# A depthwise convolution of width 31: taps on four engines, or Fourier transforms of spans of tokens on TensorE

## The chip, the cores and the metric

The kernel runs on one core of one Trainium2 chip. Times are device microseconds of one execution of the whole program. TensorE is called PE below (PEld is its weight load), VectorE is DVE, ScalarE is ACT, GpSimd is POOL, and SP is the queue that issues most transfers.

## What is computed

A two-layer encoder block over 1,024 tokens of 1,024 channels, in float32. Layer 0 mixes tokens by a convolution module, layer 1 by a gated linear recurrence, and each is followed by a squared-ReLU MLP. The change is in layer 0's convolution module:

```python
def conformer_conv(h, w_in, dw_w, dw_b, ln_g, ln_b, w_out):
    a, gate = jnp.split(h @ w_in, 2, axis=-1)
    u = a * jax.nn.sigmoid(gate)
    pad = CONV_WIDTH // 2                 # CONV_WIDTH = 31
    y = lax.conv_general_dilated(
        u, dw_w[:, None, :], window_strides=(1,), padding=[(pad, pad)],
        dimension_numbers=("NWC", "WIO", "NWC"), feature_group_count=D_MODEL)
    y = y + dw_b
    y = jax.nn.silu(layer_norm(y, ln_g, ln_b))
    return y @ w_out
# in the layer: h = rms_norm(x) * (1 + sc1) + sh1;  x = x + g1 * conformer_conv(h, ...)
#               sh1, sc1, g1, sh2, sc2, g2 = split(silu(c) @ ada_w + ada_b, 6)
```

## The kernel before

Activations lie with channels on the 128 partitions and tokens along the free axis, so x is 8 tiles of 128x1024. Every large product splits both operands into a float32r high part and the rest (`hi`/`lo`, `wh`/`wl`), and does three matmuls for one: `wh*hi`, `wh*lo`, `wl*hi`. Weights come by the SP queue into a ring of four 128x1024 tiles (`raw`), ACT rounds `wh` (line 190), and DVE, or POOL for the keys in `PW`, subtracts to get `wl` (line 194). Both go to a ring of six tiles, that is three pairs.

`start` loads x, makes the first norm and the modulation, and leaves h as 16 tiles of 128x2x512 (8 blocks of channels, two halves of 512 tokens). `conv_layer` then goes over 8 blocks of 128 channels. `conv_in(b)` makes both halves of a and gate, with weights stationary and h moving (512 columns), and writes u as three sequences: even tokens, odd tokens, and their sum (line 729, POOL), which is a two-phase split of the filter into three filters of half the length. While `conv_in(b + 1)` runs on PE, `conv_pe` and `conv_taps` apply block b's taps: some by a diagonal stationary matrix on PE (line 756, its diagonal made by ACT at line 755), the even ones by ACT's scale (line 770) and POOL's add (line 772), the odd ones and the sum's as a chain of multiply-adds on DVE (line 782, into the SBUF tile `g` and into the PSUM tile `aux`). y is put together at lines 796 and 798, and its mean over channels is summed on PE into two banks (line 800).

When all 8 blocks are done the layer norm follows: `conv_center`, `conv_rms` (squares, sums, Newton steps, spread over partitions by line 480), `conv_swish` with the split into z; then `out_proj` of the first half of the tokens, the second half's swish, and `out_proj` of the second half in `rest`, with layer 0's MLP behind it. The modulation's parts are products with ada_w: most are done as POOL products (line 382) that ACT sums (line 387), one 128x1024 tile for 128 outputs; g1, part (0, 2), is done on PE by `ada_pe` (line 409). Part (0, 4) is spread over the first `out_proj`, (0, 3) follows it.

Instructions are put in order by a planner from the program's order, priorities and estimated costs, engine by engine; `keep_in_program_order` pins one to its place. PSUM has 3 banks for `acc`, 3 for `aux` and 2 for `mu` in this layer.

Of the kernel before, what the change touches and what calls it, by code (L numbers as in the profile page):

```python
# [13 lines left out]
P = 128  # L14
D = 1024
# [7 lines left out]
NE = KW // 2 + 1  # L23
UW = T // 2 + PAD
# [16 lines left out]
TAPS = [(2, 16, 0)] * 6 + [(3, 16, 5), (16, 13, 0)]  # L41
# [30 lines left out]
PW = [("ci", 0, 0), ("ci", 0, 1), ("co", 3), ("co", 4)]  # L72
ADA_PE = [(0, 2)]
# [12 lines left out]
class K:  # L86
    def __init__(self, tc, ins, out):
        self.tc, self.nc, self.ins, self.out = tc, tc.nc, ins, out
        self.uid = self.ndg = 0
        self.pin = self.pins = self.stay = False  # L90
        self.turn = {"acc": 0, "aux": 0}
        self.pq = self.kept = None
# [22 lines left out]
    def plan(self):  # L115
# [12 lines left out]
        for b in range(NB):  # L128
            L.append((("ci", b, 0), [col(w_in, b)], "std"))
            L.append((("ci", b, 1), [col(w_in, NB + b)], "std"))  # L130
# [30 lines left out]
    def fetch(self, upto):  # L161
        while self.fnext <= min(upto, len(self.wlist) - 1):
            key, aps, _ = self.wlist[self.fnext]
            self.raws[key] = []
            for ap in aps:
                raw = self.raw()
                self.nc.sync.dma_start(out=raw.rearrange("p (k n) -> p k n", n=ap.shape[-1]), in_=ap)
                self.raws[key].append(raw)
            self.fnext += 1

    def prep(self, upto):
        while self.wnext <= min(upto, len(self.wlist) - 1):
# [3 lines left out]
            self.wready[key] = {"std": self.prep_std, "spill": self.prep_std, "again": self.prep_again,  # L176
                                "pair": self.prep_pair}[kind](key, aps, raws, kind)
# [7 lines left out]
    def prep_std(self, key, aps, raws, kind):  # L185
# [4 lines left out]
        i = nc.scalar.copy(out=wh, in_=raw)  # L190
        if self.stay:
            self.tc.keep_in_program_order(i)
        eng = nc.gpsimd if key in PW else nc.vector
        i = eng.tensor_tensor(out=wl, in0=raw, in1=wh.bitcast(F32), op=ALU.subtract)
        if self.stay and eng is nc.gpsimd:
            self.tc.keep_in_program_order(i)
# [108 lines left out]
    def setup_late(self):  # L305

        nc, cp = self.nc, self.cp
        self.dw = cp.tile([P, NB, KW], F32, name="dw")
        nc.sync.dma_start(out=self.dw, in_=self.ins["dw"].rearrange("p (b k) -> p b k", k=KW))
        self.dws = cp.tile([P, NB, NE], F32, name="dws")  # L310
        nc.vector.tensor_tensor(out=self.dws[:, :, 0:NE - 1], in0=self.dw[:, :, 0:KW - 1:2], in1=self.dw[:, :, 1::2],
                                op=ALU.add)
        nc.vector.tensor_copy(out=self.dws[:, :, NE - 1:], in_=self.dw[:, :, KW - 1:])

# [53 lines left out]
    def ada(self, layer, part, cond, tile, eng="vector", late=False):  # L368

        nc = self.nc  # L370
        for b in range(NB):
# [9 lines left out]
            else:  # L381
                i = nc.gpsimd.tensor_tensor(out=raw, in0=raw, in1=cond, op=ALU.mult)  # L382
                if self.stay:
                    self.tc.keep_in_program_order(i)
# [13 lines left out]

    def ada_pe(self, layer, part, steps):


        nc = self.nc
        w = self.ins["ada_w"].rearrange("(k p) n -> p k n", p=P)
        ps = [self.acc() for _ in range(2)]
        for k in range(NB):
            raw = self.hp.tile([P, D], F32, tag="h", name=self.nm("raw"))
            nc.sync.dma_start(out=raw, in_=w[:, k, ADA_PE.index((layer, part)) * D:][:, 0:D])
            for j in range(2):
                m = nc.tensor.matmul(ps[j][0:1], self.cond[:, k:k + 1], raw[:, self.hs(j)],
                                     start=(k == 0), stop=(k == NB - 1))  # L410
                self.tc.keep_in_program_order(m)
            if k + 1 in steps:
                yield
        yield
        rows = []
        for j in range(2):
            row = self.t512("row")[0:1]
            nc.scalar.copy(out=row, in_=ps[j][0:1])
            rows += [row[:, i * P:(i + 1) * P] for i in range(4)]
        ps = self.aux()  # L420
        for b in range(NB):
            nc.tensor.matmul(ps[:, b:b + 1], rows[b], self.ones_c[0:1], start=True, stop=True)
        self.ada_done(layer, part, ps[:, 0:NB], 0, NB)
        yield
# [132 lines left out]
    def mod_split(self, layer, n, b, t):  # L557
        shift = self.gcol(layer, 3 * n, b)
        h = self.hp.tile([P, 2, H], F32R, tag="h", name=self.nm("h"))
# [5 lines left out]
    def mod_split_pool(self, layer, n, s, b, r):  # L565

        nc = self.nc
        h = self.hp.tile([P, 2, H], F32R, tag="h", name=self.nm("h"))
# [101 lines left out]
    def start(self):  # L670
# [13 lines left out]
        h = [[], []]  # L684

        def block(b):
            for s in range(2):
                if s:
                    h[s].append(self.mod_split_pool(0, 0, s, b, rs[s]))
                else:  # L690
                    t, _ = self.mod_scale(0, 0, s, b, rs[s])
                    h[s].append(self.mod_split(0, 0, b, t)[0])
# [17 lines left out]
    def conv_in(self, b, h):  # L710


        nc, sp = self.nc, self.sp
        u = sp.tile([P, 3, UW], F32, tag="u", name=self.nm("u"))
        for i, n in ((0, PAD // 2), (1, PAD // 2 + 1)):
            nc.gpsimd.memset(u[:, i, 0:n], 0.0)
            nc.gpsimd.memset(u[:, i, n + H:], 0.0)
        ws = [self.weights(("ci", b, i), 2 if b else 0) for i in range(2)]
        for s in range(2):
            pa, pg = self.acc(), self.mu.tile([P, H], F32, tag="mu", name=self.nm("mu")) if b == 0 and s else self.acc()  # L720
            self.mm3(pa, ws[0], slice(0, P), h[s])
            self.mm3(pg, ws[1], slice(0, P), h[s])
            sg = self.t512("sg")
            nc.scalar.activation(out=sg, in_=pg, func=AF.Sigmoid)
            uv = self.view(u, PAD // 2 + s * H // 2, [[1, H // 2], [UW + 1, 2]])
            nc.vector.tensor_tensor(out=uv, in0=pa.rearrange("p (m i) -> p m i", i=2),
                                    in1=sg.rearrange("p (m i) -> p m i", i=2), op=ALU.mult)
            if s:
                nc.gpsimd.tensor_tensor(out=u[:, 2], in0=u[:, 0], in1=u[:, 1], op=ALU.add)
            yield u  # L730

    def spare(self, i):

        return self.x[i][:, self.hs(1)]

    def conv_pe(self, b, u):  # L740

        nc, sp = self.nc, self.sp
        n0, n1, late = TAPS[b]
        banks = []
        for x, w, lo, hi, more in ((u[:, 2], self.dws[:, b], 0, n0, late), (u[:, 0], self.dw[:, b, 0::2], n1, NE, 0)):
            ps = self.aux() if hi > lo else None
            self.diag(ps, x, w, lo, hi, True, not more)
            banks.append(ps)
        return banks

    def diag(self, ps, x, w, lo, hi, start, stop):
        for j in range(lo, hi):
            self.ndg += 1
            d = self.spare(2 + self.ndg % 8 // 4)[:, self.ndg % 4 * P:(self.ndg % 4 + 1) * P]
            self.nc.scalar.activation(out=d, in_=self.ident, func=AF.Copy, scale=w[:, j:j + 1])
# [826 lines left out]
```

## Time and profile before

| | us |
|---|---|
| median of 3 runs | 2584.30 (2583.52 to 2584.58) |
| the profiled execution | 2588.68 |
| its span, first to last instruction | 2586.9 |
| PE busy in the span | 2411.8 (93%) |
| DVE busy | 1955.2 (76%) |
| POOL busy | 1130.6 (44%) |
| ACT busy | 1044.7 (40%) |
| mean granted PE clock | 0.973 |

The span is read by stages, since the shares of the whole hide that different engines set the pace in different stages. A matmul's duration in the trace overlaps with the next one's; what a matmul costs a full PE is the distance from its start to the next one's start. A float32 (not float32r) matmul stands in the trace as two instructions.

### The profile page before, as it was taken

What the parts mean: (1) busy time and instruction counts of PE and PEld (TensorE: products, weight loads), DVE (VectorE), ACT (ScalarE), POOL (GpSimd) and SP (SyncE); (2) the same over time, 40 slices, a digit from 0 to 9 for tenths busy, and PEclk for the clock granted to TensorE, in tenths of its full rate; (3) what the DMA queues carried; (4) which work ended last, traced back from release to release, by engine and by line L of the source; (5) the groups of instructions that cost most, each with busy time, mean ns of one, the idle gap of its engine ahead of it and who ended that gap; (6) DMA issues with size and microseconds to landing.
All of it is one profiled execution on the core that took longest, in us unless ns stands there. A gap on an engine that the chain in (4) does not pass through costs nothing.

```text
span 2586.9 us, 31297 instructions
## 1 busy us (share of the span) xinstructions
PE 2411.8 (93%) x11538; PEld 1974.0 (76%) x11538; DVE 1955.2 (76%) x2547; ACT 1044.7 (40%) x1738; POOL 1130.6 (44%) x647
## 2 busy tenths in 40 slices
PE   3888778889899999999999999999998999999998
PEld 2666536667688878888889898988877888888887
DVE  8999989896576789765776767768669766686565
ACT  5544435343333444444433434442424333333443
POOL 4678755466576588211111101111016666564421
PEclk9998889989999999999999999999998999999999
DMA  7111422424444946552211112122522444574554
GB/s 248 41 33 33 155 104 82 164 94 159 159 159 168 339 174 227 197 179 90 74 58 50 58 58 66 58 66 65 204 98 93 157 153 139 207 271 169 188 179 154
DMA packets 214974, 347.25 MB, mean 134 GB/s; under 512 B 13091, under 2 KB 117795, under 8 KB 214822
## 3 DMA queue, kind: packets, MB, share of 16 engines
q1 hardware_dynamic: 213094, 343.17, 38.9%
q8 instruction: 90, 1.47, 0.2%
q10 hardware_dynamic: 1728, 2.10, 0.2%
q14 instruction: 62, 0.51, 0.1%
HBM read 267.62 MB, written 77.60 MB: 133 GB/s over the span
## 4 chain that ended last, share of the span: by engine, by line
PE 71%; DVE 19%; issue 4%; POOL 3%; DMA 2%; ACT 0%; SPq 0%; POOLq 0%; DVEq 0%; ACTq 0%
PE acc L267 16%; DVE g L782 5%; PE acc L956 5%; PE acc L957 5%; PE acc L952 5%; PE acc L1058 4%; PE acc L1053 4%; PE aux L1224 4%; PE acc L1057 4%; PE aux L1053 3%; PE aux L1058 3%; PE aux L1057 3%; DVE aux L782 2%; PE acc L257 2%; PE acc L258 2%
## 5 line engine op out<-in xcount | busy, mean ns | idle before, releaser
L382 POOL TENSOR_TENSOR raw<-raw,cond 128x1024 f32<-128x1024 f32 x56 | 160.2, 2863 | 549.4 <-DMA raw<-in_ada_t 466.9
L267 PE MATMUL acc<-h,wh 128*128 128x512 f32 x1024 | 328.7, 397 | 0.0
L222 DVE TENSOR_TENSOR wp<-raw,wp 128x512 fp32r<-128x512 f32 x192 | 198.7, 1043 | 115.0 <-ACT wp L221 114.5
L952 PE MATMUL acc<-h,wp 128*128 128x512 f32 x640 | 254.4, 403 | 11.4 <-ACT wp L221 8.3
L956 PE MATMUL acc<-h,wp 128*128 128x512 f32 x640 | 256.8, 402 | 7.6 <-DVE h L629 7.6
L957 PE MATMUL acc<-h,wp 128*128 128x512 f32 x640 | 255.3, 404 | 5.4 <-DVE wp L222 5.4
L221 ACT CAST wp<-raw 128x512 fp32r<-128x512 f32 x192 | 117.2, 620 | 353.9 <-PE acc L957 183.9
L1041 DVE TENSOR_TENSOR o<-hold,o 128x1024 fp32r<-128x1024 f32 x80 | 156.2, 1953 | 83.8 <-ACT o L1040 76.8
L267 PEld LDWEIGHTS acc<-h,wh 128*128 128x128 f32 x1024 | 190.5, 189 | 37.0
L267 PE MATMUL acc<-h,wl 128*128 128x512 f32 x512 | 202.9, 397 | 0.0
L1058 PE MATMUL acc<-o,o 128*128 128x512 f32 (+1 forms) x512 | 195.2, 383 | 2.9 <-DVE o L1041 2.9
L1057 PE MATMUL acc<-o,o 128*128 128x512 f32 (+1 forms) x512 | 194.2, 379 | 0.0
L1053 PE MATMUL acc<-o,o 128*128 128x512 f32 (+1 forms) x512 | 194.0, 382 | 0.0
L772 POOL TENSOR_TENSOR x<-x,x 128x512 f32<-128x512 f32 x117 | 183.3, 1566 | 8.2
L1041 DVE TENSOR_TENSOR o<-c,o 128x1024 fp32r<-128x1024 f32 x96 | 174.6, 1819 | 12.6 <-ACT o L1040 12.5
L1053 PE MATMUL aux<-o,o 128*128 128x512 f32 (+1 forms) x448 | 171.0, 382 | 0.4 <-ACT o L1040 0.4
L1057 PE MATMUL aux<-o,o 128*128 128x512 f32 (+1 forms) x448 | 169.1, 377 | 0.0
L1058 PE MATMUL aux<-o,o 128*128 128x512 f32 (+1 forms) x448 | 167.1, 380 | 0.6 <-DVE o L1041 0.6
L952 PEld LDWEIGHTS acc<-h,wp 128*128 128x128 f32 x640 | 123.9, 194 | 43.3 <-ACT wp L221 10.9
L1040 ACT CAST o<-hold 128x1024 fp32r<-128x1024 f32 x80 | 83.9, 1049 | 172.1 <-issue 86.5
L957 PEld LDWEIGHTS acc<-h,wp 128*128 128x128 f32 x640 | 123.5, 193 | 37.0 <-DVE wp L222 8.9
L956 PEld LDWEIGHTS acc<-h,wp 128*128 128x128 f32 x640 | 123.3, 193 | 36.6 <-DVE h L629 8.4
(257 smaller groups left out, 6232.5 us busy)
## 6 DMA issues: line engine op xcount, KB each, us to landing
raw<-in_mlp_w SPq DMA_DIRECT2D x144, 512.0 KB, 4.4
c<-hid SPq DMA_DIRECT2D x112, 512.0 KB, 3.5
hid<-c SPq DMA_DIRECT2D x128, 256.0 KB, 3.1
raw<-in_ada_t SPq DMA_DIRECT2D x56, 512.0 KB, 3.7
hid<-t SPq DMA_DIRECT2D x96, 256.0 KB, 2.9
raw<-in_hgrn_w_in SPq DMA_DIRECT2D x40, 512.0 KB, 3.8
aw<-in_ada_t SPq DMA_DIRECT2D x32, 512.0 KB, 7.9
hold<-in_mlp_w SPq DMA_DIRECT2D x32, 512.0 KB, 7.8
```

Source lines behind the costliest of these rows:

```text
L222: nc.vector.tensor_tensor(out=lo, in0=a, in1=hi.bitcast(F32), op=ALU.subtract)
L267: m = self.nc.tensor.matmul(ps, a, b, start=(k == 0 and i == 0), stop=(k == n - 1 and i == 2))
L382: i = nc.gpsimd.tensor_tensor(out=raw, in0=raw, in1=cond, op=ALU.mult)
L772: nc.gpsimd.tensor_tensor(out=e, in0=e, in1=p, op=ALU.add)
L782: nc.vector.scalar_tensor_tensor(out=out, in0=x[:, j:j + n], scalar=w[:, j:j + 1], in1=out, op0=ALU.mult, op1=ALU.add)
L952: m = nc.tensor.matmul(ps, wh, hi, start=(k == 0 and i not in (3, 6, 7)), stop=False, skip_group_check=True)
L956: nc.tensor.matmul(ps, wh, lo, start=False, stop=False, skip_group_check=True)
L957: nc.tensor.matmul(ps, wl, hi, start=False, stop=(k == KH - 1), skip_group_check=True)
L1041: nc.vector.tensor_tensor(out=lo, in0=src, in1=hi.bitcast(F32), op=ALU.subtract)
L1053: m = nc.tensor.matmul(ps[j], wh[:, c], hi, start=first, stop=False, skip_group_check=True)
L1057: nc.tensor.matmul(ps[j], wh[:, c], lo, start=False, stop=False, skip_group_check=True)
L1058: nc.tensor.matmul(ps[j], wl[:, c], hi, start=False, stop=stop, skip_group_check=True)
```

## The change

The tap loops and their three sequences go. Tokens of u are now on partitions, in 8 tiles of 128 tokens, and channels go in 4 groups of 256 (`G`). For a half of 512 tokens, three spans (`NWIN`) of 171 output tokens (`DV`) are each computed from 201 input tokens by a transform of length 202 (`DN`), whose 102 frequencies lie on partitions: cosine and sine sums by matmuls with fixed matrices (`F`), a complex product with the filter's transform (`W`), and an inverse by matmuls with fixed matrices (`Gm`), after which y is again channels by tokens.

`conv_in(ps, g)` has h stationary and the weights moving (256 columns of a and 256 of gate), and holds one bank for each 128 tokens. It runs in two passes over all 1,024 x 2,048 weights: pass 0 for tokens 0 to 639 (5 tiles), pass 1 for 640 to 1023 (3 tiles). The weights are therefore loaded, rounded and subtracted twice. u of tiles 3 and 4 is kept for pass 1. `forward` and `backward` of a group are put between the four quarters (`kp`) of the next group's `conv_in`. The first half's layer norm and swish (`conv_norm`) go one step per quarter into pass 1; the second half's go into the first `out_proj`. The matrices F and the kept u take the place of x in SBUF, so all of x is loaded again behind the last `forward`. `ada_pe` goes; parts (0, 2), (0, 4) and (0, 3) all become POOL products through the ring `raw`, in pass 1 and the first `out_proj`.

The diff, cut:

```diff
-TAPS = [(2, 16, 0)] * 6 + [(3, 16, 5), (16, 13, 0)]
+DN = 202
+DV = 171
+NWIN = 3
+G = 256
+NG = D // G
+PASS = [range(0, 5), range(5, 8)]
+KEPT = [3, 4]
+SHIFTS = [(j, t) for j in range(NWIN) for t in range(-1, 5)
+          if any(0 <= P * t + p - DV * j + PAD < DV + KW - 1 for p in range(P))]
...
-PW = [("ci", 0, 0), ("ci", 0, 1), ("co", 3), ("co", 4)]
-ADA_PE = [(0, 2)]
+PW = [("ci", 0, 0, 0), ("ci", 0, 0, 1), ("co", 3), ("co", 4)]
...
+        for ps in range(len(PASS)):
+            for g in range(NG):
+                for k in range(0, NB, 2):
+                    L.append((("ci", ps, g, k // 2), [w_in[:, k + i, :, g * G:(g + 1) * G] for i in range(2)], "whole"))
...
     def setup_late(self):
+        xr = [self.xp.tile([P, T], F32R, tag="x", name=self.nm("xr")) for _ in range(NB)]
+        self.F = [xr[i][:, 0:H].rearrange("p (e c f) -> p e c f", e=2, c=2) for i in range(n)]
+        self.ukept = [t[:, H:].rearrange("p (e n) -> p e n", e=2) for t in xr]
+        for i in range(n + 2):
+            if i % 4 == 0:
+                raw = self.raw()
...
+            nc.scalar.copy(out=hi, in_=src)
+            nc.vector.tensor_tensor(out=lo, in0=src, in1=hi.bitcast(F32), op=ALU.subtract)
...
+    def conv_in(self, ps, g, h, U):
+        banks = {t: self.acc() if i < 3 else self.mbank() for i, t in enumerate(PASS[ps])}
+        for kp in range(NB // 2):
+            wh, wl = self.weights(("ci", ps, g, kp))
+            for k in range(2 * kp, 2 * kp + 2):
+                a, b = (w[:, self.hs(k % 2)] for w in (wh, wl))
+                for t, bank in banks.items():
+                    c = slice(t % 4 * P, (t % 4 + 1) * P)
+                    hi, lo = (h[t // 4][k][:, e, c] for e in range(2))
+                    nc.tensor.matmul(bank, hi, a, start=(k == 0), stop=False)
+                    nc.tensor.matmul(bank, hi, b, start=False, stop=False)
+                    nc.tensor.matmul(bank, lo, a, start=False, stop=(k == NB - 1))
+            if kp < NB // 2 - 1:
+                yield
+        for t, bank in banks.items():
+            w = self.t512("u")
+            nc.scalar.activation(out=w[:, 0:G], in_=bank[:, G:], func=AF.Sigmoid)
+            nc.vector.tensor_tensor(out=w[:, G:], in0=bank[:, 0:G], in1=w[:, 0:G], op=ALU.mult)
...
+            nc.scalar.copy(out=u[:, 0], in_=w[:, G:])
+            nc.vector.tensor_tensor(out=u[:, 1], in0=w[:, G:], in1=u[:, 0].bitcast(F32), op=ALU.subtract)
...
+    def forward(self, s, g, U):
+        for j in range(NWIN):
+            ps = self.aux()
+            ts = [(i, 4 * s + t) for i, (w, t) in enumerate(SHIFTS) if w == j and 0 <= 4 * s + t < NB]
+            for c in range(2):
...
+                    nc.tensor.matmul(out, fh, hi, start=(n == 0), stop=False)
+                    nc.tensor.matmul(out, fh, lo, start=False, stop=False)
+                    nc.tensor.matmul(out, fl, hi, start=False, stop=(n == len(ts) - 1))
...
+            for out, c in ((p, 0), (q, 1)):
+                w = self.W[:, c:c + 1, g * G:(g + 1) * G].broadcast_to([P, 2, G])
+                nc.vector.tensor_tensor(out=out, in0=sp, in1=w, op=ALU.mult)
+            for c, op in ((0, ALU.add), (1, ALU.subtract)):
+                nc.gpsimd.tensor_tensor(out=p[:, c], in0=p[:, c], in1=q[:, 1 - c], op=op)
...
+            self.split(y, p)
...
+    def backward(self, s, g, Y, ys, sums):
+        banks = [self.aux() for _ in range(3)]
+        for j in range(NWIN):
+            for b in range(G // P):
+                mm = [(Y[j][:, e, c, b * P:(b + 1) * P], self.Gm[:, f, c]) for c in range(2)
+                      for e, f in ((0, 0), (0, 1), (1, 0))]
...
+            if 0 < n < NB - 2:
+                nc.gpsimd.tensor_tensor(out=sums[0], in0=sums[0] if n > 1 else ys[0], in1=y, op=ALU.add)
...
+    def conv_norm(self, ys, sums, s, z):
+        for i, t in enumerate((sums[0], ys[NB - 2], ys[NB - 1])):
+            nc.tensor.matmul(mu, self.ones_d, t, start=(i == 0), stop=(i == 2))
...
     def conv_layer(self, h):
+                for ps in range(2):
+                    for g in range(NG):
+                        ci = self.conv_in(ps, g, h, U)
...
+                        go()
+                        if prev:
+                            F = self.forward(*prev, U)
+                        go()
+                        go()
+                        if prev:
+                            self.backward(*prev, F, Y[prev[0]], S[prev[0]])
+                            if prev == (0, NG - 1):
+                                norm = self.conv_norm(Y[0], S[0], 0, z[0])
+                                cond = self.cond_rows(0)
+                                gen = itertools.chain(*(self.ada(0, part, cond, self.raw, "gpsimd") for part in (2, 4, 3)))
+                        go()
+                        prev = (ps, g)
+                F = self.forward(*prev, U)
+                self.x = [self.xp.tile([P, T], F32, tag="x", name=self.nm("x")) for _ in range(NB)]
+                for s in range(2):
+                    self.load_x(s)
+                for _ in norm:
                     pass
+                self.backward(*prev, F, Y[1], S[1])
...
+                norm = self.conv_norm(Y[1], S[1], 1, z[1])
+                with tc.high_priority():
+                    for _ in range(6):
+                        next(norm)
+                def step():
+                    for _ in range(2):
+                        with tc.high_priority():
+                            next(norm, None)
+                        next(gen, None)
+                self.out_proj("co", z, 0, 0, step=step)
```

## Rows read from the trace of the kernel before

**Rows 1.** Windows: start:end, length, busy us (instructions) by engine, clock, DMA share, GB/s.

```profile
43.00:86.00 43.00, 30.43 (x106) 22.43 (x105) 38.63 (x50) 27.17 (x53) 21.28 (x23) 0.84 0.20 59
86.00:350.00 264.00, 217.75 (x779) 150.14 (x778) 260.19 (x284) 116.14 (x185) 196.63 (x145) 0.93 0.19 62
350.00:382.00 32.00, 20.71 (x63) 8.81 (x61) 25.20 (x31) 12.24 (x20) 22.64 (x15) 0.82 0.40 136
382.00:433.00 51.00, 40.54 (x154) 31.67 (x155) 47.97 (x60) 26.72 (x45) 22.17 (x9) 0.87 0.37 132
433.00:500.00 67.00, 61.55 (x267) 50.35 (x266) 56.74 (x70) 32.02 (x54) 42.61 (x26) 0.95 0.42 157
500.00:545.00 45.00, 33.40 (x114) 24.79 (x113) 40.79 (x60) 17.98 (x32) 21.09 (x12) 0.77 0.08 24
1000.00:1500.00 500.00, 495.86 (x2733) 429.17 (x2732) 367.97 (x562) 210.66 (x365) 103.36 (x37) 1.00 0.33 109
```

**Rows 2.** The chain of waits, 86 to 350 us, its shares by line.

```profile
by line: DVE g L782 45.6%; DVE aux L782 20.8%; DVE wl L194 8.2%; issue 6.8%; DVE y L798 5.5%; DVE u L726 3.4%; DVE g L780 3.3%; DVE eg L787 3.1%; DVE y L796 2.4%; PE mu L800 0.8%; DVE x L785 0.3%; DVEq L787 0.0%; DVEq L782 0.0%
```

**Rows 3.** Groups of DVE instructions, 86 to 350 us: busy us, mean ns.

```profile
L782 DVE SCALAR_TENSOR_TENSOR g<-u,dw,g 128x513 f32<-128x513 f32 x112 | 128.1, 1144 | 1.4
L782 DVE SCALAR_TENSOR_TENSOR aux<-u,dws,aux 128x512 f32<-128x512 f32 x92 | 68.6, 746 | 0.5
L194 DVE TENSOR_TENSOR wl<-raw,wh 128x1024 fp32r<-128x1024 f32 x16 | 24.9, 1556 | 0.0
```

**Rows 4.** Timeline of PE, 300 to 311 us: start, length, instructions.

```profile
300.45 0.40 PE L254 MATMUL acc<-h,wh 128*128 128x512 f32 x1
...
306.14 0.39 PE L257 MATMUL acc<-h,wh 128*128 128x512 f32 x1
...
306.60 4.45 PE L756 MATMUL aux<-u,x 128*128 128x512 f32 x10
```

**Rows 5.** Timeline of PE, 1206.8 to 1207.7 us, matmuls of 256 columns.

```profile
1206.88 0.40 PE L267 MATMUL acc<-wh,h 128*128 128x256 f32 x2
1207.12 0.28 PE L267 MATMUL acc<-wl,h 128*128 128x256 f32 x1
1207.24 0.40 PE L267 MATMUL acc<-wh,h 128*128 128x256 f32 x2
```

**Rows 6.** Groups of instructions, 0 to 640 us: busy us, mean ns.

```profile
L254 PE MATMUL acc<-h,wh 128*128 128x512 f32 x248 | 105.5, 429 | 1.9 <-ACT h L573 1.8
L800 PE MATMUL mu<-y,ones_d 128*128 128x512 f32 x32 | 20.5, 740 | 10.4 <-DVE y L796 9.9 <-DVE y L798 0.5
L409 PE MATMUL acc<-raw,cond 128*1 128x512 f32 x32 | 14.2, 592 | 0.0
L772 POOL TENSOR_TENSOR x<-x,x 128x512 f32<-128x512 f32 x117 | 183.3, 1566 | 8.2
L796 DVE SCALAR_TENSOR_TENSOR y<-aux,vec,eg 128x256 f32<-128x256 f32 x16 | 7.0, 477 | 0.1
L815 DVE TENSOR_TENSOR y<-y,mu 128x512 f32<-128x512 f32 x5 | 3.1, 682 | 2.0 <-ACT mu L808 2.0
L838 DVE SCALAR_TENSOR_TENSOR y<-y,vec,aux 128x512 f32<-128x512 f32 x16 | 11.2, 742 | 3.7 <-PE aux L480 3.7
```

**Rows 7.** Timeline of PE: behind the first `conv_in`, and the MLP's first product.

```profile
86.14 0.39 PE L258 MATMUL acc<-h,wl 128*128 128x512 f32 x1
...
499.48 0.39 PE L952 MATMUL acc<-h,wp 128*128 128x512 f32 x1
```

**Rows 8.** Timeline of POOL, DVE and PE, 459 to 464 us.

```profile
458.43 9.29 POOL L382 TENSOR_TENSOR aw<-aw,aw 128x1024 f32<-128x1024 f32 x4
458.48 7.00 DVE L479 TENSOR_SCALAR d<-ident,rw 128x128 f32<-128x128 f32 x3
...
460.91 0.49 PE L480 MATMUL aux<-d,ones_m 128*128 128x128 f32 x2 [1.75 <-DVE d L479]
```

**Rows 9.** Timeline of PE behind that wait, 466 to 468 us.

```profile
466.55 0.63 PE L257 MATMUL acc<-z,wh 128*128 128x512 f32 x1
...
467.83 0.63 PE L257 MATMUL acc<-z,wh 128*128 128x512 f32 x1
```

More of the change, by code (lines that the diff above doesn't have):

```diff
@@ L397, in ada @@
                 yield
[L399 to L424, printed above, removed]
     def ada_done(self, layer, part, src, b, n, eng=None):
@@ L683, in start @@
         g1, g0 = self.ada(0, 1, cond, tile, "vector"), self.ada(0, 0, cond, tile, "gpsimd")
-        h = [[], []]
+        h = [[self.hp.tile([P, 2, H], F32R, tag="h", name=self.nm("h")) for _ in range(NB)] for _ in range(2)]
         def block(b):
@@ L736, in spare @@
[L736 to L755, printed above, removed]
-            self.nc.tensor.matmul(ps, d, x[:, j:j + H], start=(start and j == lo), stop=(stop and j == hi - 1))
@@ L817, in conv_rms @@
-    def conv_rms(self, ys, ada=None, mid=None, late=False):
-        ps = self.aux()
-        order = sorted(range(NB), key=lambda b: b in CPOOL)
-        sq = self.sumsq([ys[b] for b in order], 3 if ada else 0, late=late)
-        self.token_sums(ps, sq)
-        if ada:
-            next(ada)
-            mid()
-        r = self.spread(self.newton(ps))
-        for _ in ada or ():
-            pass
-        return r
-    def conv_swish(self, ys, r, s):
-        nc = self.nc
-        z, ts = [], []
-        pin = lambda i: self.tc.keep_in_program_order(i) if not s else None
+        a = [None, None]
@@ L1557, in _arrays, with dft @@
     a["ada_t"] = np.ascontiguousarray(w.transpose(0, 2, 1)).reshape(2 * 6 * D, D)
-    a["ada_w"] = np.concatenate([w[l, :, p * D:(p + 1) * D] for l, p in ADA_PE], axis=1)
-    dw = np.asarray(inputs["conv_dw_w"][0]).reshape(KW, NB, P)
-    a["dw"] = np.ascontiguousarray(dw.transpose(2, 1, 0)).reshape(P, NB * KW)
+    a["dw"] = np.ascontiguousarray(inputs["conv_dw_w"][0])
+    f = np.arange(P)
+    on = f <= DN // 2
+    def dft(n, ok, scale=1.0):
+        x = 2 * np.pi / DN * np.outer(n, f)
+        return np.concatenate([ok[:, None] * on * scale * c for c in (np.cos(x), np.sin(x))], axis=1)
+    ms = []
+    for j, t in SHIFTS:
+        n = P * t + np.arange(P) - DV * j + PAD
+        ms.append(dft(n, (n >= 0) & (n < DV + KW - 1)))
+    v = np.arange(G)
+    back = dft(v, v < DV, np.where((f == 0) | (f == DN // 2), 1.0, 2.0) / DN)
+    ms += [back[:, c * P:(c + 1) * P].T for c in range(2)]
+    a["dft"] = np.concatenate(ms, axis=1).astype(np.float32)
+    a["fw"] = dft(np.arange(KW), np.ones(KW)).astype(np.float32)
     s, t = np.arange(P)[:, None], np.arange(P)[None, :]
```

244 lines of the change are left out of this document (112 added, 132 removed).

## The prediction, as it was put on record

> **What bounds the kernel now.** I read the windows by stage first [rows 1]. Up to 500 us PE is never full for long; from 1000 us on it is busy 496 of 500 us at a granted clock of 1.00. So the kernel is a PE program with a slow head, and a change in the head is worth what it moves the moment at which the MLP starts, 499.5 us [rows 7]. In the tap loop, 86 to 350 us, DVE is busy 260 of 264 us while PE has 218 in longer, lazily overlapped instructions at clock 0.93 [rows 1]. The chain of waits says the same: two thirds of it are DVE's two tap chains, line 782 into `g` and into `aux` [rows 2]. From 350 to 382 us no engine is full: that is the layer norm, a latency that nothing covers [rows 1]. From 382 to 433 us DVE leads again (48 of 51 us, swish and conversions), from 433 to 500 us PE does, but for one gap [rows 1, 8].
>
> What a matmul costs a full PE is the distance between starts. 26 matmuls of 512 float32r columns start from 300.45 to 306.14 us: 5.69 / 25 = 0.228 us. Ten float32 records fill 4.45 us with the last one's tail: about 0.43 us each [rows 4]. Three of 256 columns take 1207.24 - 1206.88 = 0.36 us: 0.120 each [rows 5].
>
> **What PE must do from 86 us to the MLP, after the change.** I take 86 us as common mark [rows 7], since `start` and the arrival of h are not touched.
> - `conv_in`: the count is unchanged, 8 token tiles x 4 groups x 8 k x 3 = 768 of 512 columns (before 16 blocks x 2 halves x 8 x 3). Before, 96 were done at the mark. After, the first group has 120 that wait for h, which comes one k at a time; the last k leaves 15, 3.4 us, so I count all 120 as done (if only 96: +5.5 us). Left: 648 x 0.228 = 147.7 us.
> - Transforms: `SHIFTS` has 8 pairs of span and tile, of which a half uses 7, so `forward` has 7 x 2 x 3 = 42 and `backward` 3 x 2 x 6 = 36 matmuls of 256 columns. 8 group-halves x 78 x 0.120 = 74.9 us. This is the main addition.
> - Means: 2 x 3 float32 products are 12 records x 0.43 = 5.2 us. Token sums and spreads stay, some 4.5 us. The filter's transform (4 float32 products, 3.4 us) fits in PE's gaps before the mark, 43 us with 30 busy [rows 1].
> - `out_proj`: 2 x 192 x 0.228 = 87.5 us, unchanged.
>
> Sum 319.8 us. Gone are 78 diagonal records (39 taps), 32 of `mu` and 32 of `ada_pe` [rows 4, 6]: 142 x 0.43 = 61 us. PE's own work thus grows by about 19 us; the gain has to come from the 103 us that PE now loses between the mark and the MLP (413.3 us less 672 + 384 matmuls, 240.8, 61 and 8 of small ones).
>
> **What the others must do.** DVE's taps (128 + 69 us) go [rows 3]. In their place, for one group: four conversions x 1.56 = 6.2 us [rows 3]; per token tile a product from PSUM of 256 columns, 0.48 as line 796 has it [rows 6], and a subtraction, half of the 1.14 us of a 512-wide DVE instruction with both inputs in SBUF [rows 3], 0.57; six spectrum products from PSUM x 0.68 [rows 6] = 4.1; three splits x 1.14 = 3.4. In pass 0 (5 tiles) that is 19 us of DVE under 120 x 0.228 + 78 x 0.120 = 36.7 us of PE. In pass 1 (3 tiles) it is 16.9, and a quarter of the first half's norm: 5 centrings x 0.68, 5 sums, 8 swishes and 4 splits x 1.14, 8 scalings x 0.74, 3 us of Newton and spread: 31.8 / 4 = 7.9. Together 24.8 us under 72 x 0.228 + 9.4 = 25.8 us of PE. Pass 0 is PE's with room; pass 1 is a near tie.
>
> POOL in a pass-1 group: six half-wide products of `forward` x 0.78, half of line 772's [rows 6] = 4.7, sums of y 2.0, norm 3.5, and 13 / 4 modulation tiles x 2.3 [rows 8] = 7.5: 17.7 us. The modulation's 8 extra tiles (g1, before on PE) are covered by this room; without it they would cost 8 x 2.3 = 18 us ahead of the first residual.
>
> POOL and DVE disturb each other. Into `aux`, which lies in PSUM, a tap takes 0.746 us; into `g`, with both inputs in SBUF, 1.144 [rows 3]; and three DVE instructions that run beside four POOL products of ada last 7.00 us, while PE waits for them [rows 8]. The Trainium skill, "SBUF — State Buffer", section "SBUF: two separate sides", says that the two engines share one pair of ports by an exclusive lock held for a whole instruction: the loser stands still. The rows agree. By the rule in full, a pass-1 group would need POOL's 17.7 us plus DVE's locked part; that is the second rival below.
>
> SP's queue gets 64 weight pieces of 256 KB where 16 of 512 KB were, 8 modulation tiles for 8 of `ada_w`, and 16 pieces of x where 8 were. A load that waits for a `raw` slot holds the weights behind it; in pass 1 four weight tiles and three modulation tiles share four slots. F takes two slots until x is free, near 80 us. The residuals' x comes only behind the last `forward`; three banks of 24 matmuls, 16 us, cover it.
>
> **Stalls that I allow.** Pass 0: 1.5 us a group, for the hand-over of the five banks (sigmoid, then product) before the next group's first matmul: 6 us. Nothing before shows it; it can be 0 (the bank freed first has 2.7 us before the last matmul ends) or one conversion late, 1.56 x 2 = 3 us. Pass 1: 4 us a group, the same and the wait for u and Y behind a DVE that is nearly full: 16 us (bounds 0 and 9, the DVE sum a third too low). The last group's tail: 4 us. Between the halves of `out_proj`: the second norm takes about what the first took, 32 us [rows 1], and its swish as long as PE's 44 us allow; 6 us (0 to 20). The wait for the spread in `out_proj`, unchanged: 6 us [rows 8]. Sum 38 us.
>
> 319.8 + 38 = 358 us from the mark, against 413: the MLP starts 55 us earlier, near 444 us. Behind it nothing is changed, so all 55 us reach the end. Against the profiled execution's own 2588.7 us that gives 2533.7; it was 4.4 us above the median, so 2529 us.
>
> **Rivals.**
> 1. *Hardly any stall.* PE runs the passes as it runs 1000 to 1500 us. Only half of the allowances stay or fewer, and modulation that is ready earlier shortens the 11 us that PE lacks between 500 and 545 us [rows 1]. 19 + up to 11 us more: 2499 to 2512, in the extreme 2485. For it: DVE has 17 us of room in each pass-0 group. Against: every group has two hand-overs between four engines.
> 2. *The locked ports set pass 1.* Locked DVE work in a group is conversions, u, splits and 4.8 of the norm, 16.1 us at the disturbed durations; alone it is near 11. 11 + 17.7 = 28.7 us against 25.8, and behind it the in-order queues pay twice: I price 4 x (2.9 + 4) more, and 8 us in the first `out_proj`, where DVE has norm, conversions and residuals. 36 us of the gain go: 2565, from 2545. The Trainium skill's lock is this case. Against: the unlocked DVE work can lie beside POOL.
> 3. *Slower: the transforms' chain is not covered.* u, `forward`, products, POOL's sums, split, `backward` are one dependent chain per group. If PE waits for each of the eight chains instead of working on the next group's quarters, each costs DVE 9 and POOL 5 us, 14 us against the 2.8 us that I allow a group; such waits also drop the clock to a spacing of 1.28 / 3 = 0.427 us [rows 9]. It decides from 55 / 8 = 6.9 us a group above my allowance, 9.6 in all. 8 x 11 = 90 us: 2620. Against it: two quarters, 13.7 us in pass 0 and 8.2 in pass 1, lie between `forward` and `backward`.
> 4. *No change.* The gain is eaten exactly, at the same 9.6 us a group, or the MLP cannot start earlier since its first weights or part (0, 3) come late. Both parts are now loaded earlier, so little speaks for it: 2580 to 2589.
>
> **How the numbers follow.** Forecast 0.55 (its own range 2508 to 2546), rival 1 0.15, rival 2 0.18, rival 3 0.08, rival 4 0.04. The range 2490 to 2566 holds the forecast and most of rivals 1 and 2, about 0.82. A change of 0.2% (5 us) is what a measurement here can tell. Faster: 0.55 + 0.15 + 0.18 = 0.88; slower 0.08; same 0.04.
>
> **What would show it.** In the windows: PE near full at clock 1.00 from 90 us to the second `out_proj`; pass 0 about 38 us a group and pass 1 about 30; DVE no longer the chain's leader in pass 0. The MLP's first product near 444 us, and the same distance from there to the end as before. It is wrong if matmuls of 256 columns with their own weight load cost more than 0.120 us, if PE waits for Y or u more than 5 us a group, or if the second `out_proj` waits long for z.

## The result, and the profile after

The changed kernel takes 2524.18 us, the median of 4 runs (2522.93 to 2526.26), beside 2584.10 of the kernel before (4 runs): ratio 0.9769, 95% interval 0.9752 to 0.9786. That is 60 us faster, 5 us more than forecast. On another chip it took 2528.88 beside 2583.16, ratio 0.9792 (0.9775 to 0.9809). So some 5 us between runs on two chips mean nothing; lengths of stages up to the MLP's start, which repeated within 2 us, are compared below where such differences matter.

The head of the page of the kernel after, with its slices of PE and of the granted clock:

```profile
span 2524.5 us, 32142 instructions
PE 2414.2 (96%) x12024; PEld 2019.9 (80%) x12024; DVE 1819.7 (72%) x2440; ACT 1015.9 (40%) x1722; POOL 1008.4 (40%) x554
...
PE   4999898899999999999999999999989999999998
...
PEclk9899898899999999999999999999999999999999
```

PE is busy for 2414 us as before (2412), in a span 62 us shorter. The work was not made less; holes were closed. Where they were is read from the windows by stage, cut at the last matmul of pass 0 (203.6 us), the last of pass 1 (327.9), and the MLP's first product (columns as in [rows 1]):

```profile
86.00:204.00 118.00, 118.00 (x611) 100.36 (x611) 47.26 (x75) 37.42 (x73) 23.99 (x24) 0.97 0.24 77
204.00:328.00 124.00, 114.64 (x622) 99.22 (x621) 96.00 (x122) 63.96 (x117) 72.66 (x49) 0.93 0.40 130
328.00:454.00 126.00, 112.84 (x504) 90.89 (x503) 98.36 (x131) 55.66 (x94) 68.90 (x41) 0.93 0.53 185
454.00:797.00 343.00, 325.56 (x1364) 258.79 (x1363) 259.24 (x291) 124.48 (x215) 218.28 (x135) 0.98 0.45 153
1117.00:1772.00 655.00, 652.76 (x4095) 586.89 (x4094) 479.77 (x919) 271.59 (x571) 86.34 (x38) 1.00 0.21 65
```

Pass 0 is what the change promised: PE without a gap, DVE at 47 of 118 us where it had 260 of 264 [rows 1]. In pass 1 and behind it PE has holes, the granted clock falls to 0.93, and DVE and POOL together are busy for 169 and 167 us of 124 and 126.

The timeline of PE, first behind the mark of 86 us, then in pass 0, then where the MLP starts:

```profile
88.16 0.63 PE L727 MATMUL acc<-wl,h 128*128 128x512 f32 x1
88.59 0.63 PE L726 MATMUL acc<-wh,h 128*128 128x512 f32 x1
...
92.14 1.39 PE L345 MATMUL aux<-raw,fw 31*128 31x512 f32 x2
...
93.79 0.40 PE L727 MATMUL mu<-wl,h 128*128 128x512 f32 x1
...
133.39 0.39 PE L728 MATMUL acc<-wh,h 128*128 128x512 f32 x1
133.62 0.28 PE L759 MATMUL aux<-u,xr 128*128 128x256 f32 x1
133.74 0.40 PE L726 MATMUL acc<-wh,h 128*128 128x512 f32 x1
133.98 0.39 PE L727 MATMUL acc<-wl,h 128*128 128x512 f32 x1
...
453.99 0.39 PE L272 MATMUL acc<-z,wl 128*128 128x512 f32 x1
454.22 0.39 PE L962 MATMUL acc<-h,wp 128*128 128x512 f32 x1
```

A matmul of the transforms (line 759, 256 columns) takes 133.74 - 133.62 = 0.12 us, as in [rows 5], also with a weight load of its own. The MLP starts at 454.2 us, 45.3 earlier than before [rows 7] and 10 later than forecast.

The chain of waits by line, first of pass 0 (86 to 204 us), then of pass 1 (204 to 328 us):

```profile
by line: PE acc L726 15.2%; PE acc L727 15.0%; PE acc L728 15.0%; PE aux L784 11.0%; PE mu L726 10.0%; PE mu L727 9.8%; PE mu L728 9.6%; PE aux L760 4.3%; PE aux L761 4.3%; PE aux L759 4.2%; PE aux L345 1.8%
...
by line: DMA raw<-in_ada_t 25.4%; POOL raw L415 16.8%; issue 13.3%; DVE wl L208 7.4%; POOL p L768 6.5%; PE acc L726 4.4%; PE acc L727 4.1%; DVE sg L839 3.6%; PE acc L728 3.6%; ACT wh L206 2.5%; DVE Y L289 2.4%; DVE q L766 2.1%; ACT raw L418
```

In pass 0 every step is a matmul. In pass 1 the chain runs through the modulation: a transfer of ada_t, POOL's product on it (line 415), the next transfer. The waits of POOL in pass 1 (us in total, times, longest) and those of PE say how this reaches the matmuls:

```profile
POOL raw L415 <- DMA raw<-in_ada_t: 40.9, 10, 9.7
```

```profile
PE aux L784 <- DVE Y L289: 4.9, 2, 3.9
PE acc L726 <- DVE u L734: 2.5, 2, 2.2
PE aux L784 <- ACT Y L288: 2.0, 1, 2.0
```

POOL stands 41 of 124 us before a modulation tile that has not arrived, and the sums of `forward`'s products (line 768) stand behind it in the same queue. PE itself waits 9.4 us in all, for Y and for u. The mean granted clock of the pass is 0.93: by this some 17 of its 124 us went at 1.2 GHz, the lower of the clock's two levels, not at 2.4 GHz, and the rest of what the pass loses is put down to that.

**The 17 us behind the MLP's start.** From the MLP's first product to the end of the last output product, the kernel before takes 2073.0 us and the one after 2055.8, in code that the diff does not touch. Ten are in layer 0's MLP, up to its first output product (352.3 before, 342.4 after; line 454:797 above), eight in the recurrence (662.5 and 654.9; line 1117:1772). Again of the kernel before and of the one after, in other runs (below), this stretch took 2072.8 and 2055.6 us, so the 17 us are no noise; 5 us in such a stretch can be, as the runs on this question show below.

### The profile page after: what moved, and what is told of

Read it like the earlier page. It is cut to its first block, busy times and chain, and to the rows that moved or that the text cites. A ratio compares the mean times of both kernels' runs of the same rounds, so it can differ in the third digit from the quotient of the medians.

```text
span 2524.5 us, 32142 instructions
## 1 busy us (share of the span) xinstructions
PE 2414.2 (96%) x12024; PEld 2019.9 (80%) x12024; DVE 1819.7 (72%) x2440; ACT 1015.9 (40%) x1722; POOL 1008.4 (40%) x554
## 4 chain that ended last, share of the span: by engine, by line
PE 75%; DVE 10%; DMA 5%; POOL 5%; issue 3%; ACT 1%; SPq 0%; POOLq 0%; DVEq 0%; ACTq 0%
PE acc L281 17%; PE acc L967 5%; PE acc L966 5%; PE acc L962 5%; PE aux L1234 4%; PE acc L1068 4%; PE acc L1063 4%; PE acc L1067 4%; PE aux L1063 3%; PE aux L1068 3%; PE aux L1067 3%; POOL raw L415 2%; DMA raw<-in_ada_t 2%; PE aux L962 2%; PE aux L966 2%
## 5 line engine op out<-in xcount | busy, mean ns | idle before, releaser
L235 ACT CAST wp<-raw 128x512 fp32r<-128x512 f32 x192 | 117.6, 621 | 349.7 <-PE acc L967 184.8
L1051 DVE TENSOR_TENSOR o<-c,o 128x1024 fp32r<-128x1024 f32 x96 | 179.9, 1874 | 12.3 <-ACT o L1050 12.2
L208 DVE TENSOR_TENSOR wl<-raw,wh 128x1024 fp32r<-128x1024 f32 x84 | 112.7, 1342 | 92.7 <-ACT wh L206 89.3
L206 ACT CAST wh<-raw 128x1024 fp32r<-128x1024 f32 x88 | 92.0, 1048 | 176.5 <-PE acc L281 116.5
L962 PEld LDWEIGHTS acc<-h,wp 128*128 128x128 f32 x640 | 122.3, 191 | 42.2 <-ACT wp L235 7.6
L966 PEld LDWEIGHTS acc<-h,wp 128*128 128x128 f32 x640 | 122.4, 191 | 37.4 <-DVE h L633 9.4
```

Of the source, the lines that this page charges most:

```text
L235: nc.scalar.copy(out=hi, in_=a)
L962: m = nc.tensor.matmul(ps, wh, hi, start=(k == 0 and i not in (3, 6, 7)), stop=False, skip_group_check=True)
L966: nc.tensor.matmul(ps, wh, lo, start=False, stop=False, skip_group_check=True)
L1051: nc.vector.tensor_tensor(out=lo, in0=src, in1=hi.bitcast(F32), op=ALU.subtract)
```

## The experiments

Each ratio is to the kernel before on the same chip: 2582.55 us (13 runs) for e1 to e4, 2584.32 (7) for e6 to e8, 2583.16 (7) for e9 to e11, 2586.28 (7) for e12. They stand in the order of the questions.

**Are the lengths of stages to be trusted?** Two plain repetitions, e5 of the kernel before and e11 of the one after.

> The kernel before, profiled once more. Its stages are the measure of what one profile's stage can tell: first MLP to the MLP's second product 352.3 us and recurrence 662.5 us in the first profile. Theory, the stages behind the convolution differ by order of work: both repeat within 2 us. Rival, they differ from run to run by as much as the changed kernel's 342.4 and 654.9 us do.

The kernel before, a single run of 2586.60 us beside 2584.32 (7 runs): MLP's start 497.7 us (499.5), its first part 353.3 (352.3), recurrence 661.0 (662.5).

> The changed kernel again, on the same chip as the two runs above: 2524 us if it repeats, and the lengths of pass 0, pass 1 and of the stretch from there to the MLP (118, 124, 126 us) within 1.5 us.

The kernel after: 2528.88 us; pass 0 ends at 202.4 us (203.6), pass 1 lasts 124.6 (124.3), the stretch from there to the MLP 128.1 (126.3). The last of the three misses its bound of 1.5. Stages up to the MLP repeat within 2 us; the whole, between chips, only within some 5 us.

**Is pass 0 PE's, and pass 1 not?** e3 keeps one of the three products in the transforms.

```diff
-                    nc.tensor.matmul(out, fh, hi, start=(n == 0), stop=False)
-                    nc.tensor.matmul(out, fh, lo, start=False, stop=False)
-                    nc.tensor.matmul(out, fl, hi, start=False, stop=(n == len(ts) - 1))
+                    nc.tensor.matmul(out, fh, hi, start=(n == 0), stop=(n == len(ts) - 1))
# and in backward
-                      for e, f in ((0, 0), (0, 1), (1, 0))]
+                      for e, f in ((0, 0),)]
```

> The changed kernel with one of the three products in both transforms, 208 matmuls of 256 columns in place of 624; the low parts are still made and not used, so the convolution is less exact. Theory, PE sets both passes: 416 x 0.120 = 50 us less of PE, of which nearly all shows: 2474 to 2485 us. Rival, other engines set pass 1: only pass 0 and the tail follow, 19 to 27 us: about 2500 us.

2497.66 us, ratio 0.9674 (0.9660 to 0.9689). Pass 0 ends 21.8 us earlier, at 181.8. Three of its groups' transforms have 3 x 52 matmuls fewer, at 0.12 us 18.7: all of it came back. Pass 1 takes 114.6 us, 9.7 shorter, where 4 x 52 x 0.12 = 25 us of PE work are gone, and the rest to the MLP 124.9, hardly shorter. Windows of its two passes:

```profile
86.00:182.00 96.00, 96.00 (x452) 79.85 (x451) 47.15 (x74) 35.96 (x73) 25.90 (x24) 0.99 0.30 94
182.00:296.00 114.00, 89.61 (x410) 72.41 (x409) 96.15 (x120) 62.49 (x113) 75.18 (x49) 0.88 0.44 135
```

Pass 1 without a third of its matmuls is 114 us long with DVE at 96, as with them: there other engines set the pace. The time is the rival's, about 2500 us.

**What does the modulation cost where the change puts it?** e4 is without it.

```diff
-                                cond = self.cond_rows(0)
-                                gen = itertools.chain(*(self.ada(0, part, cond, self.raw, "gpsimd") for part in (2, 4, 3)))
+                                gen = iter(())
+                                nc.vector.memset(self.mod[:, 0, 2:5], 0.5)
+                                nc.vector.memset(self.AB[:, 0, 1], 1.0)
```

> The changed kernel without the 24 POOL products for modulation parts 2, 4 and 3 of layer 0, their transfers and sums; constants stand in their place. Theory, POOL's work and its tiles in the ring raw disturb pass 1 and the first out_proj: of the 40 us that PE loses there (20 and 20) 15 to 25 us go, 2499 to 2509 us. Rival, the chains from bank to u to Y and the hand-over of banks: less than 5 us go, 2519 us or more.

2495.50 us, ratio 0.9664 (0.9649 to 0.9678). Pass 0 is unchanged, pass 1 takes 109.7 us (14.6 less), the stretch to the MLP 109.9 (16.4 less). Its windows of these two stretches, and below them groups of DVE instructions in pass 1:

```profile
204.00:312.00 108.00, 106.58 (x617) 93.05 (x616) 82.56 (x119) 50.05 (x89) 39.22 (x36) 1.00 0.29 91
312.00:422.00 110.00, 105.27 (x505) 86.36 (x504) 81.82 (x130) 44.01 (x73) 34.62 (x26) 1.00 0.46 156
```

```profile
L208 DVE TENSOR_TENSOR wl<-raw,wh 128x1024 fp32r<-128x1024 f32 x16 | 20.1, 1253 | 11.5 <-ACT wh L206 11.0 <-PE aux L759 0.5
L289 DVE TENSOR_TENSOR Y<-p,Y 128x512 fp32r<-128x512 f32 x12 | 11.8, 985 | 0.4
L766 DVE TENSOR_TENSOR p<-aux,W 128x512 f32<-128x512 f32 x12 | 8.2, 682 | 0.4 <-PE aux L761 0.4
```

The same groups of the changed kernel in its pass 1:

```profile
L208 DVE TENSOR_TENSOR wl<-raw,wh 128x1024 fp32r<-128x1024 f32 x16 | 27.5, 1717 | 8.7 <-ACT wh L206 8.7
L289 DVE TENSOR_TENSOR Y<-p,Y 128x512 fp32r<-128x512 f32 x12 | 15.7, 1310 | 2.2 <-ACT Y L288 1.8
L766 DVE TENSOR_TENSOR p<-aux,W 128x512 f32<-128x512 f32 x12 | 8.1, 679 | 3.7 <-POOL p L768 3.7
```

With POOL's modulation beside it the weight subtraction takes 1717 ns in place of 1253 and the split 1310 in place of 985; the spectrum product, which reads PSUM, takes 679 and 682. These are the port locks of the prediction, in one stage with and without the modulation's products. The Trainium skill, "SBUF — State Buffer", section "SBUF: two separate sides", has DVE shut out for a whole instruction when both its inputs lie in SBUF and a GpSimd instruction holds the ports; this pair of views agrees, the row with one input in PSUM included. In one pass the longer durations are 16 x 0.46 + 12 x 0.33 = 11 us of DVE. Among the 16 subtractions of the changed kernel the split is plain: the seven that met no POOL instruction took 1.22 us each, the nine that met one 2.10 us in the mean and up to 3.41.

Both stretches together are 31 us shorter, more than the 15 to 25 us of the theory; the end is 28.7 us earlier. Two runs split this. e6 leaves out POOL's products and keeps transfers, slots and ACT's sums; e7 keeps the products, as subtractions on the resident tile, and leaves out transfers and slots:

```diff
# e6
-                nc.gpsimd.tensor_tensor(out=raw, in0=raw, in1=cond, op=ALU.mult)
+                if late or part < 2:
+                    nc.gpsimd.tensor_tensor(out=raw, in0=raw, in1=cond, op=ALU.mult)
# e7
-            raw = tile()
+            here = not late and part >= 2
+            raw = cond if here else tile()
...
-            nc.sync.dma_start(out=raw, in_=self.ins["ada_t"][o * P:(o + 1) * P, :])
+            if not here:
+                nc.sync.dma_start(out=raw, in_=self.ins["ada_t"][o * P:(o + 1) * P, :])
...
-                nc.gpsimd.tensor_tensor(out=raw, in0=raw, in1=cond, op=ALU.mult)
+                nc.gpsimd.tensor_tensor(out=raw, in0=raw, in1=cond, op=ALU.subtract if here else ALU.mult)
```

> The changed kernel without POOL's 24 products for modulation parts 2, 4 and 3; their transfers into the ring raw and ACT's sums stay (of the unmultiplied weights). Theory, POOL's products hold up DVE and POOL's own queue: nearly as fast as without the modulation, 2496 to 2503 us. Rival, the transfers and the slots of the ring hold up the weights: 2515 us or more.

2502.97 us, ratio 0.9685 (0.9670 to 0.9699); pass 1 takes 117.3 us (7.0 less), the MLP starts at 431.7 (22.5 earlier). The time is the theory's.

> The changed kernel with POOL's 24 products and ACT's sums on one tile that is already there, without the 24 transfers and slots of the ring. Theory, POOL's products: near the changed kernel, 2515 to 2525 us. Rival, the ring: 2496 to 2503 us.

2512.40 us, ratio 0.9721 (0.9699 to 0.9743); pass 1 takes 121.5 us (2.8 less), the MLP starts at 437.5 (16.7 earlier). The time lies between the two expectations. So 21 us go when the products go and 12 when the transfers go, against 28.7 for both; by the MLP's start, 22.5 and 16.7 against 32.3, since e7 loses 5 us again behind it. POOL's products are the larger part, and the two overlap.

The longer durations go with the products: the subtraction takes 1299 ns in e6 and 1549 in e7, the split 915 and 1261. What POOL's 41 us of waits for transfers cost by themselves is not shown. Without transfers pass 1 is only 2.8 us shorter, but there POOL waits 16.9 us for ACT instead, since all products of e7 share one tile.

**Is it better on DVE?** e8 makes the same products there.

```diff
-                                gen = itertools.chain(*(self.ada(0, part, cond, self.raw, "gpsimd") for part in (2, 4, 3)))
+                                gen = itertools.chain(*(self.ada(0, part, cond, self.raw, "vector") for part in (2, 4, 3)))
```

> The changed kernel with the 24 products and their sums in one DVE instruction each (1.22 us, as line 379 of the kernel before has it) in place of POOL's 2.4 to 2.8 us and ACT's 1.25 us. Theory, POOL's products: faster by 5 to 15 us, since pass 1 has 13 of them, 16 us more of DVE but none of POOL's 36; 2509 to 2519 us. Rival, DVE is then the bound of pass 1 and of the first out_proj: 2524 to 2540 us. If the ring's slots were it, the shorter stay of a tile gives about half, 2510 us.

2521.74 us, ratio 0.9761 (0.9744 to 0.9777), against 0.9769 and 0.9792 of the changed kernel: no difference that can be told, and a time between the two expectations. In the profiled execution, the fastest of the four, pass 1 gains 3 us and the MLP starts at 446.5. The modulation is out of POOL's queue and its products no longer lengthen DVE's other work as they did (the subtraction takes 1385 ns, the split 1003), but DVE was the fuller engine: it is busy for 100.8 of pass 1's 121.3 us, and a modulation product takes 1447 ns there.

**Does DVE's own sum set pass 1?** The weights are rounded and subtracted twice in the new scheme. In e10 the subtraction is left out in pass 1:

```diff
+        if kind == "whole" and key[1] == 1:
+            return wh, wh
```

> In pass 1 the low part of the 16 weight tiles is not made: the high part is used in its place (less work on DVE, the same on PE; the sums are other ones). DVE has 16 x 1.5 = 24 us less in pass 1. Theory of the prediction's near tie (DVE sets pass 1, so loading and subtracting the weights twice costs what DVE takes for it): pass 1 gets 10 us shorter or more, 2512 or below. Rival (pass 1 waits for the ring and for POOL, not for DVE's sum): under 4 us, 2520 to 2525.

2512.54 us, on the same chip as the repetition at 2528.88: 16.3 us less. Pass 1 takes 116.1 us, 8.5 shorter, between the two expectations and nearer the first; the stretch behind it is 5.0 shorter. So DVE's subtraction does count in pass 1, beside POOL. How it counts is not told apart: the edit also gives a slot of `raw` back as soon as ACT has rounded, and leaves less DVE work that POOL can lengthen.

**Is the cost one of place?** Pass 0 has DVE and POOL free. Parts (0, 2) and (0, 4) go there in e9, all three, and on DVE, in e12:

```diff
-        out = self.sp.tile([P, D], F32, tag="cond", name=self.nm("cond"), bufs=1) if bufs else self.ada_tile(bufs)
+        out = self.raw() if bufs == "raw" and self.pq is None else self.sp.tile([P, D], F32, tag="cond", name=self.nm("cond"), bufs=1) if bufs else self.ada_tile(bufs)
...
+                        if (ps, g) == (0, 1):
+                            cnd = self.cond_rows("raw")
+                            early = itertools.chain(*(self.ada(0, part, cnd, self.raw, "gpsimd") for part in (2, 4)))
...
+                            if not ps and g:
+                                for _ in range(2 if g == 1 else 1):
+                                    next(early, None)
...
-                                gen = itertools.chain(*(self.ada(0, part, cond, self.raw, "gpsimd") for part in (2, 4, 3)))
+                                gen = self.ada(0, 3, cond, self.raw, "gpsimd")
# e12, against e9, cut
-                            early = itertools.chain(*(self.ada(0, part, cnd, self.raw, "gpsimd") for part in (2, 4)))
+                            early = itertools.chain(*(self.ada(0, part, cnd, self.raw, "vector") for part in (2, 4, 3)))
-                                for _ in range(2 if g == 1 else 1):
+                                for _ in range(2):
-                                cond = self.cond_rows(0)
-                                gen = self.ada(0, 3, cond, self.raw, "gpsimd")
```

> Parts (0, 2) and (0, 4) of the modulation are made in pass 0 (from its second group on, 16 tiles; their cond tile takes one of the four slots of the ring), only part (0, 3) stays in pass 1. Theory (the modulation is dear only because it was put where DVE, POOL and the ring have no room; pass 0 has it: POOL 8 and DVE 17 of 40 us): two thirds of the 28.7 us that leaving it out gave come back, about 19 us: 2505, pass 1 near 113 us, pass 0 at most 3 us longer. Rival (three slots are too few, the weights wait behind modulation tiles in pass 0 as they do in pass 1): pass 0 gets 10 to 25 us longer, 2515 to 2530.

2513.23 us, ratio 0.9729 (0.9713 to 0.9745), 15.6 below the repetition on the same chip. The stretch to the MLP takes 111.6 us (16.5 less), pass 1 116.0 (8.6 less), but pass 0 ends 8.5 us later. Both had a part: the place was worth 25 us, pass 0 took a third of it back. That the ring took it is not shown, since POOL's products lengthen DVE's work in pass 0 as well (the subtraction takes 1792 ns where it took 1225, the split 1297 for 873).

> All three parts of the modulation (24 tiles) are made in pass 0, two tiles a quarter from its second group on, by DVE in one multiply and sum in place of POOL's product and ACT's sum; pass 1 and the first output projection have none. Theory (what the modulation costs is a matter of the place, and a tile gives its slot of the ring back sooner if DVE does it alone): pass 1 near 110 us and the stretch from there to the MLP near 110 us, as without modulation; pass 0 5 to 12 us longer than 118: 2501 to 2510. Rival (24 tiles through three slots, beside 12 weight tiles, hold the weights back; DVE adds 24 x 1.2 = 29 us to its 53 in the three groups): pass 0 25 us longer or more, 2515 to 2525.

2507.01 us, ratio 0.9700 (0.9683 to 0.9718). Its windows of pass 0, pass 1 and the rest to the MLP:

```profile
86.00:210.00 124.00, 115.18 (x601) 97.96 (x600) 78.72 (x152) 35.47 (x68) 29.39 (x24) 0.96 0.53 174
210.00:320.00 110.00, 108.53 (x626) 94.70 (x625) 84.92 (x125) 52.02 (x93) 38.63 (x35) 1.00 0.27 86
320.00:432.00 112.00, 107.23 (x506) 88.08 (x505) 82.01 (x130) 44.78 (x75) 35.32 (x26) 0.98 0.45 156
```

As in its theory, pass 1 lasts 109.7 us and the stretch behind it 111.6, nearly what they are without any modulation (109.7 and 109.9); pass 0 ends at 211.2 us, 9 later than in the repetition (202.4). This version is faster than both kernels: its interval lies below both of the changed kernel's.

**Where do the 17 us behind the MLP's start come from?** One thing that crosses from the convolution into the code behind it is the counters that turn through the banks of `acc` and `aux`. They stand at 1 and 3 when `rest` begins before the change, at 0 and 1 after it, and the planner orders the same instructions by the banks that they use. Two runs set them at the start of `rest`: e1 in the kernel before to what they are after, e2 the other way round:

```diff
     def rest(self, z):
         tc, nc = self.tc, self.nc
+        self.turn = {"acc": 0, "aux": 1}      # in the kernel before; {"acc": 1, "aux": 3} in the changed one
```

> The kernel before, with the two counters that rotate acc and aux through their banks set, at the start of the part behind the convolution, to the values that the changed kernel has there (0 and 1 in place of 1 and 3). Theory, the turn of the banks: the 17 us that the changed kernel wins behind the MLP's first product (10 us in the first MLP, 7.6 us in the recurrence) come from another order of untouched work, which the planner makes from these counters; the time falls by 17 us to about 2567 us. Rival, the modulation: the first MLP is faster because POOL's products for it were done earlier; then only the recurrence's 7.6 us go, 2576.5 us. Second rival: neither, 2584 us.

The kernel before becomes faster: 2573.77 us (10 runs) beside 2582.55 (13), ratio 0.9967 (0.9957 to 0.9976), 8.8 us, with a start of the MLP that is the same (500.5). From there to the last output product it takes 2061.4 us, 11.5 less. The time lies between the theory's and the rival's; but the first part of the MLP takes 344.3 us (352.3) with the modulation as it was, so the rival's reason does not hold here.

> The changed kernel, with the two counters set at the same place to the values of the kernel before (1 and 3 in place of 0 and 1). Theory, the turn of the banks: 17 us slower, about 2541 us. Rival, the modulation: 7.6 us slower, 2532 us. Second rival: 2524 us.

The changed kernel: 2531.91 us, ratio 0.9810 (0.9789 to 0.9830); against 0.9769 and 0.9792 that is 5 to 11 us of loss, with an interval that overlaps the second one's. From the MLP's start it takes 2060.8 us, where the changed kernel has 2055.8 and 2055.6. The time is the rival's number, but not for the rival's reason: the MLP's first part is longer too (345.2 us for 342.4).

What 5 us in this stretch are worth, three runs say that leave the counters alone. In e3, e8 and e9 PE, DVE, ACT and POOL execute the same instructions in the same order from the MLP's first product on, and the stretch takes 2060.2, 2054.8 and 2061.2 us. So neither e2's 5 us nor the 5.7 us by which e1 stays above the changed kernel are evidence of anything; e1's 11.5 us, and the 8.8 us of its median, are. In the kernel before the counters thus make some 9 to 11 of the 17 us. But e2 does not bring them back: with 1 and 3 in both, the two kernels still differ by 12.1 us, and PE's order is not the same in them. More than the counters sets the order, and what else does stays open.

## Why the prediction was right, and where it was not

**The bound.** Right. The head of the kernel was DVE's, and taking the taps away moved the MLP's start and with it the end.

**The terms of the sum.** Right: 0.12 us for a matmul of 256 columns; DVE in a pass-1 group 96.0 / 4 = 24.0 us where 24.8 were worked out; POOL 72.7 / 4 = 18.2 for 17.7; POOL's half-wide product 0.87 for 0.78. DVE's sum was right because it was priced with durations disturbed by POOL (1.56 and 1.14 us); without the modulation DVE has 82.6 / 4 = 20.6 us a group. The transforms' PE cost in pass 0 came back in full in the run with one product. So pass 0 is PE's and pass 1 the near tie that was forecast.

**The stalls allowed.** Here the sum was mis-sized: 48 us for 38. PE's work from the mark to the MLP was taken as 319.8 us, and the MLP came 368.2 us behind the mark. By stage, with the prediction's own terms (half of the means and the small ones in each half): pass 0 had 110.2 us of work and took 117.6, a loss of 7.4 where 6 were allowed; pass 1 had 108 and took 124.3, 16.3 where 16 were; the rest had 101.7 and took 126.3, 24.6 where tail, hand-over and spread had 16. Two of the sizes were right by luck. That for pass 0 was meant for the hand-over of banks, but PE has no gap there (118.00 of 118.00 us). The loss lies in its first 8 us: some 15 matmuls of the first group and the end of the filter's transform, which the sum has before the mark, run there at a spacing of 88.59 - 88.16 = 0.43 us, that of the lower clock [rows 9]. From 94.0 us on, the 110.2 us of work end at 204.2, as they did. That for pass 1 was meant for hand-overs and for u and Y, and without modulation pass 1 loses 2 us only; with it, PE waits for Y and u for 9 us in four groups.

**The step that failed** is the one that costs the modulation at nothing: "The modulation's 8 extra tiles (g1, before on PE) are covered by this room". POOL's busy sum had the room, but a tile does not cost POOL's busy time alone. It holds POOL's queue until the transfer lands (41 us of waits in pass 1), takes a slot from the weights, and lengthens DVE's SBUF instructions by a third. Leaving all three parts out gives 31 of the 48 us back; up to the MLP's start the products are worth 22.5 us and the transfers with their slots 16.7, and how much of either is lock, queue or slot was not separated. How much the 8 new tiles make, apart from the 16 that the kernel before had in its first `out_proj`, was not measured by itself either; e9, which leaves 8 tiles in place, takes 8 us more over the two stretches than e4 (116.0 + 111.6 and 109.7 + 109.9).

**"Behind it nothing is changed, so all 55 us reach the end"** failed too, in the other direction: 17 us more came from code that the diff does not name. The two errors, 10 us late at the MLP and 17 early behind it, cancel in part, and it is luck that the time came nearer than its steps.

**The rivals.** Hardly any stall: not this kernel, but near what passes 0 and 1 do once the modulation is elsewhere. That its time then lies within this rival's 2499 to 2512 us (2507) it owes in part to the 17 us behind the MLP's start, of which the rival knew nothing. Locked ports: the mechanism is shown in pass 1, with 11 us of DVE, but not the price of 36 us: the whole modulation, of which the locks are a part, is worth 31. The uncovered chain: refuted, PE waits 9 us for Y and u in the four groups of pass 1 and has no gap in pass 0. No change: refuted.

## What to carry to other kernels

A background task is placed by what it holds, not by the busy share of the engine that runs it: ask which queue stands behind it, which buffer slots it takes, and whose ports. Moving 24 such tiles one stage ahead, to where PE alone sets the pace, and to DVE was worth some 17 to 22 us (16 of them moved ahead on POOL: 16 us), while moving them to DVE in the same stage was worth nothing that could be told. And before saying that code behind a change is unchanged, look for state that a scheduler carries across (here two counters of banks).

## What the runs showed of the hardware

- DVE's SBUF instructions lengthen by a third in the mean beside POOL's 128x1024 products (1253 to 1717 ns and 985 to 1310), while a DVE instruction that reads PSUM keeps its 0.68 us. Over one pass this was 11 us of DVE. A subtraction that met no POOL instruction took 1.22 us.
- Holes of a few us came with a lower clock: in pass 1 PE idled for 9.4 of 124 us with a mean granted clock of 0.93; without the modulation it idled for 1.4 of 108 at 1.00. The pass got 14.6 us shorter, more than the 8 us of idle time that went.
- Another bank at the start of a rotation, and with it another order of the same instructions by the planner, was worth 8.8 us of 2582 (0.33%). With one and the same order on four engines, a stretch of 2055 us still took up to 6 us more in single executions.
